# Gate and up projections of a feed-forward: 256 weight columns with weights stationary, against 512 columns token by token with a transposed product

## The chip, the cores and the metric

The kernel runs on one core of one Trainium2 chip. Its time is the device time of one execution in microseconds (us), a median over runs; the profile shows one execution. TensorE (PE) multiplies into PSUM, ScalarE (ACT) and VectorE (DVE) read PSUM and SBUF, GpSimd (POOL) works here on SBUF alone, and SyncE (SP) issues most DMAs. Each engine takes its instructions in a fixed order.

## The reference

Two layers over x of 256 tokens by 1024 features, in float32. Each layer has a feed-forward, a mixer and a second feed-forward:

```python
def swiglu(x, w_gate, w_up, w_down):
    return (jax.nn.silu(x @ w_gate) * (x @ w_up)) @ w_down

for l in range(DEPTH):                      # DEPTH = 2
    x = x + 0.5 * swiglu(rmsnorm(x, ffn1_norm[l]), ffn1_gate[l], ffn1_up[l], ffn1_down[l])
    ...                                     # h @ w_in, three token mixers, gates, w_out: x = x + merged @ w_out
    x = x + 0.5 * swiglu(rmsnorm(x, ffn2_norm[l]), ffn2_gate[l], ffn2_up[l], ffn2_down[l])
```

Gate and up are 1024 by 2816, down is 2816 by 1024. So four feed-forwards run, each with 8.65 million weights read once from HBM.

## The kernel before

**Numbers in two parts.** Each float32 operand is split into a rounded high part and a low rest. `mm3` (L105 to L108) makes one product from three matmuls: high by high, high by low, low by high. The first operand of each is stationary in the array, the second moves through it.

**Weights as units.** `units` lists all weight blocks in the order of use, 512 KB each. `load_unit` (L206) issues the DMA of one into a `raw` buffer (four of them, RB); `emit_unit` (L213) makes `wh` on ScalarE (L221) and `wl = raw - wh` on VectorE (L228; in other parts of the program GpSimd takes a share at L225 or L230). Five buffers hold `wh` and five `wl` (WB_); the last four units of a feed-forward have their own four, `xh` and `xl`. `unit()` asks for four units ahead.

**The feed-forward** (`ffn`, L332) goes in steps of 256 of the 2816 columns, eleven steps, `NB`. Step 0 has tokens stationary (`tok_mm`), and its product is transposed on TensorE (L361). Every later step calls `chan_mm` (L303) for gate and for up: the weights are stationary, 128 columns at a time, and all 256 tokens move, so the result has columns on the partitions. A unit is used by 24 matmuls in a row and then free. ScalarE takes silu out of PSUM (L367), VectorE multiplies by up (L369), ScalarE and GpSimd split the product into `ah` (L370) and `al` (L371). The down product (`rows_mm`, L315) of step j - 2 follows, 512 columns at a time, into four PSUM accumulators `pt` and `sc`. The PSUM tag `mm` has two buffers, `p2` and `y` one each.

**What sets the order.** The program is written in one order, and a list scheduler with a cost model of its own places instructions on each engine by priority; weight splits have a raised one. During the first feed-forward of a layer `side(j)` emits pieces of the setup of the S5 mixer (`setup_s5_layer`, L509): VectorE products at L568 to L592, GpSimd products at L584 and L586, some transposes and DMAs.

## Time and profile before

| | |
|---|---|
| median of 3 runs | 1356.99 us (1355.2 to 1362.29) |
| the profiled execution | 1357.2 us, of it the span from first to last instruction 1355.4 us |
| granted TensorE clock | 0.996 of full speed over the span |
| busy: PE, PE weight loads | 1331.6 us, 1256.8 us |
| busy: DVE, ACT, POOL | 826.8, 699.8, 465.3 us |
| HBM | 244.92 MB read, 194 GB/s over the span |

Busy time of PE counts each matmul from start to a modelled end, and matmuls overlap in the array, so a matmul shown with 0.28 us may be followed by the next 0.12 us later. What one matmul costs in a dense stream is the distance from its start to the start of the next. In a row for a window stand its length, then the busy time and count of PE, weight loads, DVE, ACT and POOL, then the granted clock, the busy share of the DMA engines and GB/s.

### The profile page before, as it was taken

Reading aid. Unit: us, or ns where it says so; the run is one execution under the profiler, and the core shown is the slowest. Engines: PE = TensorE matmul, PEld = TensorE weight load, DVE = VectorE, ACT = ScalarE, POOL = GpSimd, SP = SyncE. Lnnn points to the kernel's source line nnn. Section 1 sums busy time; section 2 is a strip of 40 time slices with the busy share of each in tenths; the row PEclk is TensorE's granted clock in tenths of the full one; section 3 lists DMA queues with packets and bytes.
Section 4 is the critical chain, followed back from the end, with each engine's and each line's share of the span. In section 5 each row is a group of like instructions: output and inputs, shape, how many; then the busy total and the mean of one; then the engine's idle time right before and its main releaser. Section 6 shows DMA issues by size and latency. Waiting matters only on the chain.

```text
span 1355.4 us, 25390 instructions
## 1 busy us (share of the span) xinstructions
PE 1331.6 (98%) x10120; PEld 1256.8 (93%) x10120; DVE 826.8 (61%) x1172; ACT 699.8 (52%) x1020; POOL 465.3 (34%) x333
## 2 busy tenths in 40 slices
PE   8999999999999999999999999999999999999998
PEld 7999988999999989999999999889999999899997
DVE  5696755996433665444675586569864337544443
ACT  5444445677644544444544444457766355544442
POOL 1442565454246531111122247254532555111110
PEclk9999999999999999999999999999999999999999
DMA  8866688666657556666756677766766576466662
GB/s 249 224 188 214 223 267 235 198 184 191 184 134 226 172 171 204 186 187 187 236 154 203 202 231 240 243 201 176 194 193 178 157 221 194 155 188 186 186 187 94
DMA packets 246326, 265.68 MB, mean 196 GB/s; under 512 B 51136, under 2 KB 224192, under 8 KB 246208
## 3 DMA queue, kind: packets, MB, share of 16 engines
q1 hardware_dynamic: 244400, 260.40, 64.7%
q10 hardware_dynamic: 1808, 3.67, 0.8%
q8 instruction: 79, 1.29, 0.4%
q14 instruction: 39, 0.32, 0.1%
HBM read 244.92 MB, written 18.58 MB: 194 GB/s over the span
## 4 chain that ended last, share of the span: by engine, by line
PE 76%; DVE 9%; DMA 7%; POOL 3%; ACT 2%; issue 2%; SPq 0%; ACTq 0%; DVEq 0%; POOLq 0%
PE mm L108 17%; PE mm L106 17%; PE mm L107 17%; PE pt L108 3%; PE pt L107 3%; PE pt L106 3%; DVE wl L228 3%; PE sc L108 3%; PE sc L107 3%; PE sc L106 3%; DMA raw<-in_w_in_dram 2%; DMA raw<-in_ffn_down_dram 1%; DMA raw<-in_ffn_gate_dram 1%; DMA raw<-in_ffn_up_dram 1%; PE pt L820 1%
## 5 line engine op out<-in xcount | busy, mean ns | idle before, releaser
L228 DVE TENSOR_TENSOR wl<-raw,wh 128x1024 fp32r<-128x1024 f32 (+3 forms) x376 | 443.5, 1186 | 340.8 <-ACT wh L221 327.2
L221 ACT ACTIVATE wh<-raw 128x1024 fp32r<-128x1024 f32 (+2 forms) x396 | 414.2, 1048 | 453.8 <-PE mm L107 240.8
L108 PE MATMUL mm<-hTh,wl 128*128 128x256 f32 x1728 | 490.7, 284 | 0.0
L107 PE MATMUL mm<-hTl,wh 128*128 128x256 f32 x1728 | 490.7, 284 | 0.0
L106 PE MATMUL mm<-hTh,wh 128*128 128x256 f32 x1728 | 489.0, 283 | 0.0
L106 PEld LDWEIGHTS mm<-hTh,wh 128*128 128x128 f32 x1728 | 326.5, 189 | 2.2
L108 PEld LDWEIGHTS mm<-hTh,wl 128*128 128x128 f32 x1728 | 325.9, 189 | 0.6 <-issue 0.3
L107 PEld LDWEIGHTS mm<-hTl,wh 128*128 128x128 f32 x1728 | 325.2, 188 | 1.3 <-issue 0.3
L371 POOL TENSOR_TENSOR al<-aa,ah 128x512 fp32r<-128x512 f32 x40 | 71.3, 1781 | 456.8 <-ACT ah L370 456.8
L230 POOL TENSOR_TENSOR wl<-raw,wh 128x384 fp32r<-128x384 f32 (+2 forms) x108 | 144.9, 1347 | 174.7 <-ACT wh L221 142.3
L106 PE MATMUL mm<-wh,hTh 128*128 128x256 f32 (+1 forms) x496 | 142.9, 290 | 0.0
L107 PE MATMUL mm<-wl,hTh 128*128 128x256 f32 (+1 forms) x496 | 141.8, 288 | 0.0
L108 PE MATMUL mm<-wh,hTl 128*128 128x256 f32 (+1 forms) x496 | 140.6, 288 | 0.0
L107 PEld LDWEIGHTS mm<-wl,hTh 128*128 128x128 f32 x496 | 94.1, 190 | 1.2 <-issue 0.3
L106 PEld LDWEIGHTS mm<-wh,hTh 128*128 128x128 f32 x496 | 94.0, 190 | 1.1 <-issue 0.3
L108 PEld LDWEIGHTS mm<-wh,hTl 128*128 128x128 f32 x496 | 93.1, 189 | 1.0 <-issue 0.3
L225 POOL TENSOR_TENSOR wl<-raw,wh 128x512 fp32r<-128x512 f32 x40 | 56.5, 1434 | 53.7 <-ACT wh L221 48.4
L107 PE MATMUL pt<-wl,ah 128*128 128x512 f32 x144 | 56.4, 392 | 0.0
L108 PE MATMUL pt<-wh,al 128*128 128x512 f32 x144 | 56.4, 391 | 0.0
L108 PE MATMUL sc<-wh,al 128*128 128x512 f32 x144 | 56.3, 391 | 0.0
L106 PE MATMUL pt<-wh,ah 128*128 128x512 f32 x144 | 56.2, 390 | 0.0
L107 PE MATMUL sc<-wl,ah 128*128 128x512 f32 x144 | 56.1, 390 | 0.0
(311 smaller groups left out, 2074.7 us busy)
## 6 DMA issues: line engine op xcount, KB each, us to landing
raw<-in_w_in_dram SPq DMA_DIRECT2D x100, 512.0 KB, 4.3
raw<-in_ffn_gate_dram SPq DMA_DIRECT2D x88, 512.0 KB, 4.4
raw<-in_ffn_up_dram SPq DMA_DIRECT2D x88, 512.0 KB, 4.7
raw<-in_ffn_down_dram SPq DMA_DIRECT2D x88, 512.0 KB, 4.3
raw<-in_w_out_dram SPq DMA_DIRECT2D x16, 512.0 KB, 4.2
Gd<-xh SPq DMA_DIRECT2D x8, 512.0 KB
Ad<-xl SPq DMA_DIRECT2D x8, 512.0 KB, 5.6
x<-Ad SPq DMA_DIRECT2D x8, 512.0 KB, 5.3
```

The lines of the kernel that those rows point to most:

```text
L106: PE.matmul(o, lh, rh, start=start, stop=False)
L107: PE.matmul(o, lh, rl, start=False, stop=False)
L108: PE.matmul(o, ll, rh, start=False, stop=stop)
L221: A.activation(hv, r, AF.Copy)
L225: G.tensor_tensor(lv[:, :, cs], r[:, :, cs], hv[:, :, cs].bitcast(F32), op=ALU.subtract)
L228: V.tensor_tensor(lv[:, :, :c], r[:, :, :c], hv[:, :, :c].bitcast(F32), op=ALU.subtract)
L230: G.tensor_tensor(lv[:, :, c:], r[:, :, c:], hv[:, :, c:].bitcast(F32), op=ALU.subtract)
L371: G.tensor_tensor(al, a, ah.bitcast(F32), op=ALU.subtract)
L820: PE.transpose(pt[:, i * P:(i + 1) * P], s[:, (b0 + i) * P:(b0 + i + 1) * P], ident)
```

## The change

Step 0 of a feed-forward stays, but its transposed product is split per token block through two PSUM tiles `p2` in place of one `y`. The other 2560 columns go in five blocks of 512 (`NJ`). A unit of gate or up is now 256 rows of 512 columns (it was 512 rows of 256 columns, the same 512 KB). `wide_tok` takes four units at once: for each block of 128 tokens, tokens are stationary and 512 weight columns move, 24 matmuls into one `mm` tile. Silu and product have the same shapes as before. The product now has tokens on the partitions, so `turned` transposes it on TensorE, four 128x128 pieces for a token block, into `p2`; ScalarE makes `ah` out of PSUM and VectorE `al`, which GpSimd made before. Down of block j - 1 follows with the four units of its rows, first token block 0, then token block 1. `side` is called eleven times, where it was twelve.

```diff
+    def wide_block(w, c0):
+        for k in range(0, KD, 2):
+            units.append(kview(w, c0, 512)[:, k:k + 2, :])
...
+    def wide_tok(h):
+        us = [unit() for _ in range(4)]
+        for t in range(2):
+            tk = slice(t * P, (t + 1) * P)
+            pq = ps("mm")
+            for kk in range(KD):
+                wh, wl = us[kk // 2]
+                mm3(pq, h[0][:, kk, tk], h[1][:, kk, tk], wh[:, kk % 2, :], wl[:, kk % 2, :], kk == 0, kk == KD - 1)
+            yield pq
...
-                else:
-                    pg = chan_mm(h)
-                    A.activation(s, pg, AF.Silu)
-                    pu = chan_mm(h)
-                    V.tensor_tensor(a, pu, s, op=ALU.mult)
-                    A.activation(ah, a, AF.Copy)
-                    G.tensor_tensor(al, a, ah.bitcast(F32), op=ALU.subtract)
...
-            if 1 < j < NB:
-                us = [unit(), unit()]
-                for t in range(2):
-                    down(j - 2, t, us)
-            side(j)
...
+        def turned(j, a, t, n, tag):
+            pt = ps(tag)
+            for c in range(n):
+                PE.transpose(pt[:, c * P:(c + 1) * P], a[:, c * P:(c + 1) * P], ident)
+            p3 = pt[:, :n * P].rearrange("p (c t) -> p c t", c=n)
+            ah, al = (b[:, :, t * P:(t + 1) * P] for b in at[j])
+            A.activation(ah, p3, AF.Copy)
+            V.tensor_tensor(al, p3, ah.bitcast(F32), op=ALU.subtract)
...
+        for j in range(1, NJ + 1):
+            at[j] = tb([P, 4, SEQ], F32R, "ah", 2), tb([P, 4, SEQ], F32R, "al", 2)
+            ss, aa = [], []
+            for pq in wide_tok(h):
+                ss.append(tb([P, 512], F32, "silu", 2))
+                A.activation(ss[-1], pq, AF.Silu)
+            side(2 * j - 1)
+            for t, pq in enumerate(wide_tok(h)):
+                aa.append(tb([P, 512], F32, "aa", 2))
+                V.tensor_tensor(aa[t], pq, ss[t], op=ALU.mult)
+            turned(j, aa[0], 0, 4, "p2")
+            us = [unit() for _ in range(2 if j == 1 else 4)]
+            down(j - 1, us, 0)
+            turned(j, aa[1], 1, 4, "p2")
+            down(j - 1, us, 1)
+            side(2 * j)
```

The order of instructions is the scheduler's, so it is shown at three places, with the tile numbers in the names. The first is TensorE in the second feed-forward of layer 0, at the end of an up product (`mm_`) and the start of down (`pt_`, `sc_`). Before:

```order
L106 MATMUL mm_1052_6437<-hTh_958_5851,wh_1047_6378 128x256
L107 MATMUL mm_1052_6437<-hTl_959_5852,wh_1047_6378 128x256
L108 MATMUL mm_1052_6437<-hTh_958_5851,wl_1048_6379 128x256
L106 MATMUL pt_997_6073<-wh_1050_6408,ah_999_6075 128x512
L107 MATMUL pt_997_6073<-wl_1051_6409,ah_999_6075 128x512
L108 MATMUL pt_997_6073<-wh_1050_6408,al_1000_6076 128x512
L106 MATMUL sc_996_6072<-wh_1050_6408,ah_999_6075 128x512
```

With the change, at the end of the second token block of up:

```order
L106 MATMUL mm_1075_5980<-wh_1062_5931,hTh_959_5414 128x512
L107 MATMUL mm_1075_5980<-wl_1063_5932,hTh_959_5414 128x512
L108 MATMUL mm_1075_5980<-wh_1062_5931,hTl_960_5415 128x512
L362 MATMUL p2_1077_6007<-ident_4_67,aa_1074_5978 128x128 x4
L107 MATMUL pt_999_5639<-wl_1066_5938,ah_1001_5641 128x512
L108 MATMUL pt_999_5639<-wh_1065_5937,al_1002_5642 128x512
L107 MATMUL sc_998_5638<-wl_1066_5938,ah_1001_5641 128x512
L108 MATMUL sc_998_5638<-wh_1065_5937,al_1002_5642 128x512
L106 MATMUL pt_999_5639<-wh_1068_5943,ah_1001_5641 128x512
L106 MATMUL sc_998_5638<-wh_1068_5943,ah_1001_5641 128x512
```

The matmuls have 512 columns where they had 256, the weights have become the moving operand, and four transposes (L362) of the first token block's product stand ahead of down.

The second place is TensorE a little later, from the end of down (before) or the first unit of the next gate product (with the change). Before, one unit follows another:

```order
L106 MATMUL sc_996_6072<-wh_1054_6440,ah_999_6075 128x512
L107 MATMUL sc_996_6072<-wl_1055_6441,ah_999_6075 128x512
L108 MATMUL sc_996_6072<-wh_1054_6440,al_1000_6076 128x512
L106 MATMUL mm_1069_6541<-hTh_958_5851,wh_1057_6470 128x256
L107 MATMUL mm_1069_6541<-hTl_959_5852,wh_1057_6470 128x256
L108 MATMUL mm_1069_6541<-hTh_958_5851,wl_1058_6471 128x256
```

With the change, wh_1082 is the first unit and wh_1085 the second; mm_1105 is token block 0 and mm_1107 token block 1:

```order
L108 MATMUL mm_1105_6119<-wh_1082_6022,hTl_960_5415 128x512
L106 MATMUL mm_1105_6119<-wh_1085_6028,hTh_959_5414 128x512
L106 MATMUL mm_1107_6146<-wh_1082_6022,hTh_959_5414 128x512
L107 MATMUL mm_1107_6146<-wl_1083_6023,hTh_959_5414 128x512
L108 MATMUL mm_1107_6146<-wh_1082_6022,hTl_960_5415 128x512
```

Token block 1 now begins on the first unit when token block 0 has used only the high part of the second, and token block 0 goes on behind it.

The third place is VectorE in the first feed-forward of layer 0, among the S5 products. Before (L568 to L570 and L590 are S5 products, L369 is the product with up):

```order
L228 TENSOR_TENSOR wl_174_926<-raw_158_849,wh_173_925 128x1024
L569 TENSOR_TENSOR s5Q_191_1084<-xh_192_1085,xl_193_1086 128x64x4
L570 TENSOR_TENSOR s5Q_191_1084<-xh_192_1085,xl_193_1086 128x64x4
L228 TENSOR_TENSOR wl_177_956<-raw_161_882,wh_176_955 128x1024
L228 TENSOR_TENSOR wl_181_988<-raw_164_888,wh_180_987 128x1024
L228 TENSOR_TENSOR wl_184_1018<-raw_172_923,wh_183_1017 128x1024
L228 TENSOR_TENSOR wl_187_1051<-raw_175_953,wh_186_1050 128x1024
L369 TENSOR_TENSOR aa_170_921<-mm_178_984,silu_169_920 128x512
L228 TENSOR_TENSOR wl_190_1057<-raw_179_985,wh_189_1056 128x1024
L228 TENSOR_TENSOR wl_203_1122<-raw_182_1015,wh_202_1121 128x1024
L228 TENSOR_TENSOR wl_206_1152<-raw_185_1048,wh_205_1151 128x1024
L590 TENSOR_TENSOR xh_222_1285<-s5C0_139_734,s5Q_191_1084 128x1024
```

With the change the lines are 20 higher for the same S5 products (L588 to L590, L610), L235 is the weight split and L392 the product with up:

```order
L235 TENSOR_TENSOR wl_154_684<-raw_116_530,wh_153_683 128x1024
L588 TENSOR_TENSOR xh_193_912<-s5Q_192_911,lam_6_74 128x512
L588 TENSOR_TENSOR xl_194_913<-s5Q_192_911,lam_6_74 128x512
L235 TENSOR_TENSOR wl_157_690<-raw_146_669,wh_156_689 128x1024
L235 TENSOR_TENSOR wl_164_750<-raw_149_675,wh_163_749 128x1024
L589 TENSOR_TENSOR s5Q_192_911<-xh_193_912,xl_194_913 128x64x4
L590 TENSOR_TENSOR s5Q_192_911<-xh_193_912,xl_194_913 128x64x4
L235 TENSOR_TENSOR wl_167_756<-raw_152_681,wh_166_755 128x1024
L610 TENSOR_TENSOR xh_217_1026<-s5C0_140_649,s5Q_192_911 128x1024
L610 TENSOR_TENSOR xh_256_1239<-s5C0_140_649,s5Q_192_911 128x1024
L235 TENSOR_TENSOR wl_170_762<-raw_155_687,wh_169_761 128x1024
L392 TENSOR_TENSOR aa_175_796<-mm_174_771,silu_159_718 128x512
```

Ahead of the product with up stand six S5 rows and five splits here, where two S5 rows and five splits stood before; two of the six are the long L610.

## Rows read from the trace of the kernel before

**Rows 1.** The page, part 1: busy us, share of span and count by engine:
```profile
PE 1331.6 (98%) x10120; PEld 1256.8 (93%) x10120; DVE 826.8 (61%) x1172; ACT 699.8 (52%) x1020; POOL 465.3 (34%) x333
```

**Rows 2.** The page, part 4: the chain that ended last, by engine:
```profile
PE 76%; DVE 9%; DMA 7%; POOL 3%; ACT 2%; issue 2%; SPq 0%; ACTq 0%; DVEq 0%; POOLq 0%
```

**Rows 3.** A window of 17 us in the second feed-forward, layer 0 (us; then engines):
```profile
538.00:555.00 17.00, 17.00 (x122) 16.02 (x121) 8.04 (x8) 7.37 (x9) 1.81 (x1) 1.00 0.64 186
```

**Rows 4.** Timeline of TensorE there, one step: start us, us, instruction:
```profile
537.43 0.28 PE L106 MATMUL mm<-hTh,wh 128*128 128x256 f32 x1
...
548.95 0.39 PE L106 MATMUL pt<-wh,ah 128*128 128x512 f32 x1
...
554.43 0.28 PE L106 MATMUL mm<-hTh,wh 128*128 128x256 f32 x1
```

**Rows 5.** Timeline of TensorE, 24 down matmuls of a first feed-forward, first and next:
```profile
138.97 0.39 PE L106 MATMUL pt<-wh,ah 128*128 128x512 f32 x1
...
144.41 0.28 PE L106 MATMUL mm<-hTh,wh 128*128 128x256 f32 x1
```

**Rows 6.** Timeline of TensorE, 452-column matmuls of the mixer, first and last of 14:
```profile
222.79 0.37 PE L106 MATMUL y<-wh,hTh 128*128 128x452 f32 x1
...
225.47 0.36 PE L107 MATMUL y<-wl,hTh 128*128 128x452 f32 x1
```

**Rows 7.** Timeline of TensorE, eight transposes of a norm and what follows:
```profile
219.83 0.60 PE L278 MATMUL y<-ident,xn 128*128 128x128 f32 x4
220.27 0.60 PE L278 MATMUL p<-ident,xn 128*128 128x128 f32 x4
220.62 0.45 PE L106 MATMUL mm<-wh,hTh 128*128 128x452 f32 x1
220.91 0.37 PE L107 MATMUL mm<-wl,hTh 128*128 128x452 f32 x1
```

**Rows 8.** Timeline of TensorE, a pause in the first feed-forward:
```profile
42.87 0.28 PE L108 MATMUL mm<-hTh,wl 128*128 128x256 f32 x1
44.99 0.34 PE L438 MATMUL y<-ident,sp_raw 64*128 64x64 f32 x2 [1.84 <-DVE smT L406]
```

**Rows 9.** Waits of TensorE and of its weight loads (total us, times, longest):
```profile
PE pt L106 <- ACT ah L370: 0.5, 2, 0.3
PEld pt L108 <- POOL al L371: 1.1, 2, 0.5
```

**Rows 10.** The page, part 5: weight split (L228, L221) and product split (L371):
```profile
L228 DVE TENSOR_TENSOR wl<-raw,wh 128x1024 fp32r<-128x1024 f32 (+3 forms) x376 | 443.5, 1186 | 340.8 <-ACT wh L221 327.2
L221 ACT ACTIVATE wh<-raw 128x1024 fp32r<-128x1024 f32 (+2 forms) x396 | 414.2, 1048 | 453.8 <-PE mm L107 240.8
...
L371 POOL TENSOR_TENSOR al<-aa,ah 128x512 fp32r<-128x512 f32 x40 | 71.3, 1781 | 456.8 <-ACT ah L370 456.8
```

**Rows 11.** The tile ah: its low part split out of PSUM, ns min/median/max:
```profile
L364 DVE TENSOR_TENSOR al<-y,ah x4: 675/679/681, 33.6 to 1181.5; 128x512 fp32r<-128x512 f32 x4
```

**Rows 12.** Timeline of GpSimd and VectorE around 79 and 700 us:
```profile
79.19 2.07 POOL L584 TENSOR_TENSOR xh<-s5b,s5Q 128x1024 f32<-128x1024 f32 x1 [4.03 <-DVE s5Q L569]
...
79.36 10.37 DVE L228 TENSOR_TENSOR wl<-raw,wh 128x1024 fp32r<-128x1024 f32 x4
...
699.62 5.25 DVE L228 TENSOR_TENSOR wl<-raw,wh 128x1024 fp32r<-128x1024 f32 x2
```

**Rows 13.** Groups by shape: VectorE's 128x1024 forms (count, busy us, mean ns):
```profile
L228 DVE TENSOR_TENSOR wl<-raw,wh 128x1024 fp32r<-128x1024 f32 x262 | 340.6, 1307 | 260.8 <-ACT wh L221 253.9 <-PE mm L108 4.3
...
L590 DVE TENSOR_TENSOR xl<-s5C,s5Q 128x1024 f32<-128x1024 f32 x8 | 22.9, 2866 | 0.2 <-ACT s5C L576 0.2
```

**Rows 14.** Waits of ScalarE and of SyncE's queue:
```profile
ACT wh L221 <- PE mm L107: 240.8, 154, 3.0
SPq L210 <- DVE wl L228: 663.9, 309, 16.7
```

**Rows 15.** The page, part 6: weight loads, KB each, us to landing:
```profile
raw<-in_ffn_gate_dram SPq DMA_DIRECT2D x88, 512.0 KB, 4.4
```

More of the change, by code (lines that the diff above doesn't have):

```diff
@@ L35 @@
 DFF = 2816
-NB = DFF // 256
+NJ = (DFF - 256) // 512
 W = 256
@@ L134, in ffn_stream @@
         g, u, d = I[f"ffn{f}_gate"][l], I[f"ffn{f}_up"][l], I[f"ffn{f}_down"][l]
-        for j in range(NB + 1):
-            if j < NB:
-                deep_block(g, 256 * j)
-                deep_block(u, 256 * j)
-            if 1 < j < NB:
-                row_block(d, 256 * (j - 2))
-            if j == NB:
-                row_block(d, 256 * (NB - 2), True)
-                row_block(d, 256 * (NB - 1), True)
+        deep_block(g, 0)
+        deep_block(u, 0)
+        for j in range(NJ):
+            wide_block(g, 256 + 512 * j)
+            wide_block(u, 256 + 512 * j)
+            if j == 0:
+                row_block(d, 0)
+            else:
+                for i in range(2):
+                    row_block(d, 512 * j - 256 + 256 * i)
+        for i in range(2):
+            row_block(d, 512 * NJ - 256 + 256 * i, True)
     def mix_stream(l):
@@ L332, in ffn, with down @@
     def ffn(h, done, side):
[L333 removed]
         at = {}
[L336 to L339 removed]
+        def down(j, us, t, hfs=(0, 1)):
+            for kk, (wh, wl) in enumerate(us):
+                st, sp = (j == 0 and kk == 0), False
                 rows_mm(acc, at[j][0][:, kk, :], at[j][1][:, kk, :], t, wh, wl, st, sp, hfs)
[L342 to L378 removed]
@@ L379, in ffn @@
-        u9, u10 = [unit(), unit()], [unit(), unit()]
+        def turned(j, a, t, n, tag):
[6 more added lines that the diff above has]
+            V.tensor_tensor(al, p3, ah.bitcast(F32), op=ALU.subtract)
+        at[0] = tb([P, 2, SEQ], F32R, "ah0"), tb([P, 2, SEQ], F32R, "al0")
@@ new lines, in ffn @@
+        us = [unit() for _ in range(4)]
+        pgu = [ps("mm") for _ in range(2)]
+        for t in range(2):
+            tok_mm(h, [t], us[:2], 256, pgu[0])
+            tok_mm(h, [t], us[2:], 256, pgu[1], None if t else h[2])
+        s, a = (tb([P, 2, SEQ], F32, n, 2) for n in ("silu", "aa"))
+        with tc.high_priority():
+            for t in range(2):
+                A.activation(s[:, t], pgu[0][:, t * 256:(t + 1) * 256], AF.Silu)
+                V.tensor_tensor(a[:, t], pgu[1][:, t * 256:(t + 1) * 256], s[:, t], op=ALU.mult)
+            for t in range(2):
+                turned(0, a[:, t], t, 2, "p2")
@@ new lines, in ffn @@
+        side(0)
+        acc = acc4()
+        for j in range(1, NJ + 1):
[14 more added lines that the diff above has]
+            side(2 * j)
@@ L380, in ffn @@
+        us = [unit() for _ in range(4)]
         tr = None
@@ L382, in ffn @@
             for hf in range(2):
-                down(NB - 2, t, u9, (hf,))
-                with behind(tr if hf else None):
-                    down(NB - 1, t, u10, (hf,))
+                for kk, (wh, wl) in enumerate(us):
+                    with behind(tr if hf and kk > 1 else None):
+                        rows_mm(acc, at[NJ][0][:, kk, :], at[NJ][1][:, kk, :], t, wh, wl, False, kk == 3, (hf,))
                 tr = update(acc, t, hf, done) or tr
```

31 lines of the change are left out of this document (removed).

## The prediction, made before the changed kernel was run

> **What bounds the kernel now.** The page's first part comes first: TensorE is busy 98% of the span, VectorE and ScalarE far less [rows 1]. The chain that ended last says the same: 76% of it is TensorE's own work, 7% DMA [rows 2]. Busy time of matmuls overlaps, though, so the next view is the windows. In the second feed-forward of layer 0 one step of 256 columns takes 17.0 us, with TensorE busy for all of it at a granted clock of 1.00 (2.4 GHz), VectorE for 8.0 us, ScalarE for 7.4 and the DMA engines 0.63 [rows 3]. The timeline of that step, read by starts, shows what the time is made of: 96 gate and up matmuls of 256 columns from 537.43 to 548.95, 0.1200 us each, and 24 down matmuls of 512 columns from there to 554.43, 0.2283 us each [rows 4]. Nothing stands between them. A feed-forward is a stream of matmuls, and its time is their number by their spacing. Weights are no limit there: ScalarE waited 240.8 us for TensorE to free a weight buffer [rows 14], so units are ready early.
>
> **Fewer, longer matmuls.** Ten steps in four feed-forwards, 96 matmuls each, are 3840 matmuls of 256 columns: 460.8 us. The change does the same products in 1920 matmuls of 512 columns. At the spacing of the down product they take 1920 x 0.2283 = 438.4 us, a gain of 22.4 us. Twice 0.1200 less 0.2283 is 0.012 us, the fixed part of one matmul that each pair saves. The trace has no gate product in the new form, tokens stationary and 512 weight columns moving. The nearest in size is the down product. The nearest in form is the mixer's projection with tokens stationary and 452 columns moving: 13 distances from 222.79 to 225.47 are 0.206 us each [rows 6], by its columns 0.2335 for 512. Then the new matmuls take 448.3 us and the gain is 12.5. I take the down product, since it has the very width, and keep 12.5 as the poor end. The good end is 0.2267: 24 down matmuls of a first feed-forward, from 138.97 to 144.41 [rows 5], which gives 25.5.
>
> **Added transposes.** Five blocks by eight 128x128 transposes in four feed-forwards are 160 (step 0 had its four already). Eight transposes of a norm start at 219.83, the matmul of 452 columns behind them at 220.62, and its successor at 220.91 [rows 7]. From 219.83 to 220.91 is 1.08 us, less 0.206 for the one matmul leaves 0.874, or 0.109 each. So a transpose costs nearly what a matmul of twice its columns costs, and 160 cost 17.5 us, all on TensorE. Matmuls and transposes together gain 4.9 us.
>
> The Trainium skill (TensorE: Matmul & The Clock Gate, section Back-to-back issue gap) gives the warm spacing as N / 2.4 GHz plus 2.5 ns: 55.8, 109.2 and 215.8 ns for 128, 256 and 512 columns. By that, halving the matmuls saves 1920 x 2.5 ns = 4.8 us, the transposes cost 8.9 us, and the two lose 4.1 us together. The trace has 109, 120 and 228 ns, so the rows decide.
>
> **Waits that go.** TensorE paused from 42.87 to 44.99 for small transposes of the S5 parameters, 2.0 us beyond one matmul [rows 8]. With the change these stand behind the whole first gate product, so that pause should vanish. At the ends of the first feed-forwards the last down product waited for the two splits, 0.5 us on ScalarE's and 1.1 us on GpSimd's [rows 9]. GpSimd's took 1.78 us [rows 10], VectorE's out of PSUM takes 0.68 [rows 11], and 24 matmuls of the other token block now stand ahead of its use. Together up to 3.6 us; some may return elsewhere, so I take 3, with bounds 0 and 3.6.
>
> **Work that is moved and hidden.** Forty low-part splits go from GpSimd to VectorE: 40 x 0.68 = 27 us more for VectorE. In the quiet feed-forwards it is half idle [rows 3], so this costs nothing there. The tile `p2` is single: the second four transposes wait until ScalarE and VectorE have read the first, some 1.3 us by the splits' durations, and 33 down matmuls (7.5 us) stand between. If that cover went, TensorE itself would stand, for 1.3 us forty times. Silu and product keep shapes and numbers. The weight loads stay 66 units per feed-forward on SyncE's queue, in rows of 2 KB. `side` still gives the S5 setup its nine pieces in layer 0.
>
> **Waits that are added.** Four units are now read twice, once per token block, so none is free before the second pass. Only the fifth buffer can be filled ahead. In the second pass a unit is free after each 6 x 0.2283 = 1.37 us. Its successor needs ScalarE's 1.05 and VectorE's 1.31 us [rows 10, 13], so it is ready 3.7 us into the pass at the earliest and wanted 6.8 us into it: 3.1 us of slack. Before, the four units ahead were used at 2.88 us each (24 x 0.1200), over 8 us of slack. In the two second feed-forwards nothing disturbs VectorE, and 3.1 us is enough. In the first ones S5 work does. Beside GpSimd's 128x1024 products, four weight splits took 10.37 us in layer 0 and two took 5.25 in layer 1 [rows 12]: 5.1 and 2.6 us over the usual. An S5 product of VectorE takes 2.87 us [rows 13], and in the third order shown two of them stand in a row between two splits. At that place TensorE should lose 2 us for the slow splits and 2.6 for the pair (5.7 less 3.1), and all matmuls behind wait with it. In layer 1 the excess of 2.6 is within the slack. I take 5 us in all. The low end is 0, if the S5 work falls where units are ready. The high end is 2 us at each of the eight quarters of S5 setup, 16 us.
>
> **Sum.** -22.4 + 17.5 - 3 + 5 = -2.9 us. The profiled execution took 1357.2 us, 1355.4 of them in the span, so 1354.3; it lies 0.2 us above the median of the runs shown, and I forecast 1354 us. Its own range is 1349 to 1361. About 0.5%, 6.8 us, is what a measurement of this kernel can tell from no change: faster is below 1350.2, slower above 1363.8.
>
> **Rivals.** *A, the S5 work costs nothing.* Without the 5 us and at the good spacing: -25.5 + 17.5 - 3.6 = -11.6, 1345.6 us. For it: in the trace the same slow splits never stopped TensorE, and a list scheduler can put S5 work where units are not yet due. Against: they had over 8 us of slack there.
>
> *B, each hand-over of four units waits.* Slower than before, if loads set the pace. SyncE's queue waits for VectorE's split to free a `raw` buffer, 663.9 us in all [rows 14], so a load starts only when a split ends, and four now end in a burst. A buffer goes round in load, 1.05 and 1.31 us, and four buffers must go round once per 24 + 24 matmuls, 10.9 us. So loads may take 8.5 us before TensorE stands. Against it: they land in 4.4 us [rows 15], and even at the mean 186 GB/s of the window [rows 3], 2.8 us a unit, the fourth load of a burst, issued 4.1 us after the first, lands in 7.1. From 8.5 us on it decides. With loads of 9 us it costs 0.5 us at each of some 60 hand-overs: 1357.2 - 4.9 - 3 + 30 = 1379 us.
>
> *C, the new form spaces like the 452-column product.* -12.5 + 17.5 - 3 + 5 = +7.0, 1364 us. For it: the same form, on the same engine. Against: the down product, at the full width, keeps 0.228 in every feed-forward. (The skill's spacing rule, named above, points the same way.)
>
> **How the numbers follow.** Forecast 0.55, A 0.25, B 0.12, C 0.08. Faster by over 0.5%: A and a little of the forecast's low end, 0.30. Slower: B and most of C, 0.19, and the forecast's high end adds 0.01: 0.20. Within 0.5%: 0.50. The range takes in A's time and C's, and on the high side stops within B: 1345 to 1369 us.
>
> **What would show it.** Starts of gate matmuls 0.227 to 0.230 us apart, and transposes 0.109, confirm the first two terms; 0.233 is C. A block of 512 columns in the second feed-forward should take 2 x 48 x 0.2283 + 0.87 + 48 x 0.2283 = 33.7 us where two steps took 34.0. New pauses of TensorE should lie between 60 and 105 us, with VectorE's split as the releaser; none at all is A. Pauses at each hand-over in the second feed-forwards, released by a split that waited for a DMA, are B, and the forecast is wrong. It is also wrong if the mixer, which the change does not touch, moves by more than 2 us because the scheduler orders it anew.

## The result and the profile after

The changed kernel takes 1370.09 us (median of 4 runs, 1367.86 to 1371.23), the kernel before in the same session 1358.17 (1355.2 to 1362.29): a ratio of 1.0095, interval 1.0072 to 1.0118. It is about 1% slower. The forecast was 1354 us and its range ended at 1369. The profiled execution spans 1368.3 us at a mean granted clock of 0.991 (before 1355.4 and 0.996), so 12.9 us are to be explained.

The page of the changed kernel, busy time and chain by engine, answers [rows 1, 2]:

```profile
PE 1341.6 (98%) x8360; PEld 1176.2 (86%) x8360; DVE 849.4 (62%) x1216; ACT 700.5 (51%) x1024; POOL 406.5 (30%) x293
...
PE 81%; DVE 9%; DMA 4%; ACT 2%; issue 2%; POOL 2%; SPq 0%; POOLq 0%; DVEq 0%; ACTq 0%
```

TensorE has 1760 instructions fewer (1920 matmuls fewer, 160 transposes more) and is as busy as ever. To see where the time went, the span is cut at the first transpose of each norm. Worked out from the traces, in us:

| | FFN 1, layer 0 | mixer | FFN 2 | FFN 1, layer 1 | mixer | FFN 2 |
|---|---|---|---|---|---|---|
| before | 205.25 | 281.13 | 188.99 | 197.63 | 280.58 | 194.24 |
| changed | 208.52 | 280.09 | 190.33 | 205.50 | 280.79 | 195.57 |

The mixers moved by -1.0 and +0.2. Every feed-forward became longer: the second ones, where nothing disturbs VectorE, by 1.3 each, the first ones by 3.3 and 7.9. These are stages of one profiled execution each. The second feed-forwards repeat within 0.7 us where nothing in them is changed (189.00 and 194.49 in e14 below, which has them as before; 190.95 and 195.62 in e6, which has them as changed). For the whole, the time of one kernel moves with the granted clock: the kernel before, run 29 times in one session, took 1353.02 us at 0.997 and 1362.45 at 0.988.

**The undisturbed loss.** The timeline of TensorE in the second feed-forward of layer 1, the counterpart of [rows 4]: the first and the 49th gate matmul of a block, and the first of the next block.

```profile
1250.96 0.40 PE L106 MATMUL mm<-wh,hTh 128*128 128x512 f32 x1
...
1262.11 0.40 PE L106 MATMUL mm<-wh,hTh 128*128 128x512 f32 x1
...
1285.16 0.40 PE L106 MATMUL mm<-wh,hTh 128*128 128x512 f32 x1
```

11.15 us for 48 steps are 0.2323 each, where I had taken the 0.2283 of the down product. A block takes 34.20 us; I had said 33.7, against 34.0 for the two steps it replaces. Five blocks make 1.0 of the 1.3 us. No wait stands in between.

**The largest new wait.** It lies in the first feed-forward of layer 1. The timeline of ScalarE and VectorE, then that of TensorE (in brackets the idle time before an instruction and its releaser), then windows with the busy time of PE, PEld, DVE, ACT and POOL, the granted clock and the DMA's share:

```profile
706.27 0.38 ACT L365 ACTIVATE ah<-p 128x256 fp32r<-128x256 f32 x1 [0.93 <-PE p L362]
703.07 5.24 DVE L235 TENSOR_TENSOR wl<-raw,wh 128x1024 fp32r<-128x1024 f32 x2
708.23 2.04 DVE L591 TENSOR_TENSOR s5D<-s5D,cm 128x128 f32<-128x128 f32 x1
710.20 6.32 DVE L610 TENSOR_TENSOR xh<-s5C,s5Q 128x1024 f32<-128x1024 f32 x2
716.45 0.41 DVE L366 TENSOR_TENSOR al<-p,ah 128x256 fp32r<-128x256 f32 x1
```

```profile
705.86 0.38 PE L362 MATMUL p<-ident,aa 128*128 128x128 f32 x2
...
712.85 0.49 PE L595 MATMUL y<-ident,s5c 128*128 128x128 f32 x3
716.91 0.44 PE L362 MATMUL p<-ident,aa 128*128 128x128 f32 x2 [3.57 <-DVE al L366]
```

```profile
713.00:717.00 4.00, 0.43 (x5) 0.20 (x3) 4.00 (x4) 1.54 (x2) 3.92 (x2) 1.00 0.00 0
...
718.00:721.50 3.50, 3.50 (x9) 2.33 (x8) 3.50 (x3) 0.35 (x1) 0.75 (x1) 0.53 0.18 32
```

The second pair of transposes of step 0 waits for the single tile `p2`, which the views call `p`. That tile is free when the 0.41 us split at 716.45 has read it. ScalarE's copy of the tile had ended at 706.65; the split then stood 9.8 us in VectorE's queue, behind two weight splits of 2.6 us each, beside which GpSimd ran, and three S5 products. TensorE had 29 gate matmuls and three S5 transposes to do meanwhile, 705.99 to 713.34, and stood still for the rest. After the pause the clock is granted at about half (0.53; 1.2 GHz is one half) for 3.5 us, with 9 matmuls in a window in which the next one has 16.

**Other waits of TensorE** (in total us, times, longest), to hold against [rows 9]:

```profile
PE p L362 <- DVE al L366: 3.6, 1, 3.6
...
PE sc L106 <- DVE x L342: 2.9, 3, 2.1
...
PE mm L107 <- DVE wl L235: 1.2, 1, 1.2
```

The pause for `smT` [rows 8] is gone, as forecast. Three of these waits, in the timeline of TensorE: for a weight split in the first feed-forward of layer 0, at the end of the same one for the update of x, and at the norm behind the first feed-forward of layer 1.

```profile
144.70 0.50 PE L107 MATMUL mm<-wl,hTh 128*128 128x512 f32 x1 [1.23 <-DVE wl L235]
213.37 0.50 PE L106 MATMUL sc<-xh,ah 128*128 128x512 f32 x1 [2.12 <-DVE x L342]
891.96 0.66 PE L285 MATMUL y<-ident,xn 128*128 128x128 f32 x4 [0.93 <-DVE xn L281]
```

The end of the first feed-forward of layer 0 now waits for the update of x, where before it waited for the splits.

### The profile page after: what moved, and what is told of

Read it like the earlier page. It is cut to its first block, busy times and chain, and to the rows that moved or that the text cites. A ratio compares the mean times of both kernels' runs of the same rounds, so it can differ in the third digit from the quotient of the medians.

```text
span 1368.3 us, 21779 instructions
## 1 busy us (share of the span) xinstructions
PE 1341.6 (98%) x8360; PEld 1176.2 (86%) x8360; DVE 849.4 (62%) x1216; ACT 700.5 (51%) x1024; POOL 406.5 (30%) x293
## 4 chain that ended last, share of the span: by engine, by line
PE 81%; DVE 9%; DMA 4%; ACT 2%; issue 2%; POOL 2%; SPq 0%; POOLq 0%; DVEq 0%; ACTq 0%
PE mm L106 18%; PE mm L108 18%; PE mm L107 18%; DVE wl L235 3%; PE pt L107 3%; PE pt L108 3%; PE pt L106 3%; PE sc L108 3%; PE sc L106 3%; PE sc L107 3%; PE p L362 1%; PE pt L840 1%; PE y L966 1%; PE y L964 1%; DMA raw<-in_ffn_gate_dram 1%
## 5 line engine op out<-in xcount | busy, mean ns | idle before, releaser
L235 DVE TENSOR_TENSOR wl<-raw,wh 128x1024 fp32r<-128x1024 f32 (+3 forms) x376 | 459.8, 1232 | 292.8 <-ACT wh L228 285.6
L228 ACT ACTIVATE wh<-raw 128x1024 fp32r<-128x1024 f32 (+2 forms) x396 | 412.8, 1048 | 389.7 <-PE mm L108 185.7
L106 PE MATMUL mm<-wh,hTh 128*128 128x512 f32 (+1 forms) x1136 | 396.8, 353 | 0.2 <-ACT hTh L289 0.2
L107 PE MATMUL mm<-wl,hTh 128*128 128x512 f32 (+2 forms) x1136 | 395.3, 351 | 1.6 <-DVE wl L235 1.2
L108 PE MATMUL mm<-wh,hTl 128*128 128x512 f32 (+1 forms) x1136 | 394.6, 350 | 0.0
L107 PEld LDWEIGHTS mm<-wl,hTh 128*128 128x128 f32 x1136 | 216.5, 191 | 30.9 <-DVE wl L235 2.3
L108 PE MATMUL mm<-hTh,wl 128*128 128x256 f32 x448 | 126.7, 283 | 0.0
L107 PE MATMUL mm<-hTl,wh 128*128 128x256 f32 x448 | 126.6, 283 | 0.0
L106 PE MATMUL mm<-hTh,wh 128*128 128x256 f32 x448 | 126.4, 282 | 0.0
L107 PEld LDWEIGHTS mm<-hTl,wh 128*128 128x128 f32 x448 | 84.3, 188 | 0.3 <-issue 0.3
L108 PEld LDWEIGHTS mm<-hTh,wl 128*128 128x128 f32 x448 | 84.3, 188 | 0.3 <-issue 0.3
L106 PEld LDWEIGHTS mm<-hTh,wh 128*128 128x128 f32 x448 | 84.4, 188 | 0.0
L392 DVE TENSOR_TENSOR aa<-mm,silu 128x512 f32<-128x512 f32 x40 | 27.4, 686 | 48.4 <-PE mm L108 48.4
```

Source lines behind the costliest of these rows:

```text
L106: PE.matmul(o, lh, rh, start=start, stop=False)
L107: PE.matmul(o, lh, rl, start=False, stop=False)
L108: PE.matmul(o, ll, rh, start=False, stop=stop)
L228: A.activation(hv, r, AF.Copy)
L235: V.tensor_tensor(lv[:, :, :c], r[:, :, :c], hv[:, :, :c].bitcast(F32), op=ALU.subtract)
L392: V.tensor_tensor(aa[t], pq, ss[t], op=ALU.mult)
```

## The experiments

Every ratio is to the kernel before, run on the same chip in the same session.

**e1, streams of TensorE alone.** Is the 0.232 made by 24 matmuls in a row into one PSUM bank?

```diff
+ for j, (k, i) in enumerate(every):      # L111: one bank for 24
+     PE.matmul(o[r % 2], *terms(k)[i], start=j == 0, stop=j == 23)
...                                       # L116, L121, L127: bank changed every 3, 1, 6
+ for j in range(24):                     # L130: one bank, operands fixed
+     PE.matmul(o[2 + r % 2], *terms(0)[0], start=j == 0, stop=j == 23)
```

> The kernel holds nothing but ten streams of TensorE work on operands that lie in SBUF, each on its own line, with no other engine and no DMA at work beside them; it leaves out everything else that the two kernels compute. In the changed kernel the gate and up matmuls start 0.232 us apart and the down matmuls of the same 512 columns 0.227. Theory, the bank: a gate or up pass puts 24 matmuls in a row into one bank of PSUM, the down product three. Then the stream of 24 in a row and the one with a single stationary and a single moving operand, both in one bank, are spaced 0.232 us, the streams that change the bank after three (also with fixed operands) and after every one 0.227, after six between them; 452 columns in one bank 0.206; 256 columns with weights stationary 0.120 in one bank and a few ns less where the bank changes. Rival one, the neighbours: the gate passes lose 5 ns to reads and writes of other engines, and here all streams of 512 columns show 0.227. Rival two, the operands: fixed operands give 0.227, changing ones 0.232, whatever the bank. Transposes 0.109 in all of them.

Grouped by line: durations, and the first and last start in us.

```profile
L116 PE MATMUL b<-wh,hl x48: 389/389/389, 60.5 to 92.5; 128*128 128x512 f32 x48
...
L130 PE MATMUL b<-wh,hh x144: 389/389/389, 153.5 to 185.9; 128*128 128x512 f32 x144
```

The one-bank stream takes 32.4 us for 143 steps, 0.2266; the one that changes the bank every three, 32.0 for 141, 0.2270. Median distances of all streams of 512 columns were 226 or 227 ns, of 452 columns 0.2065 and of 256 columns 0.120. The bank has no part in it, and 452 columns cost 0.2065 with nothing beside them.

**e2, no transposes.**

```diff
-            pt = ps(tag)
-            for c in range(n):
+            pt = ps(tag) if j == 0 else a
+            for c in range(n if j == 0 else 0):
                 PE.transpose(pt[:, c * P:(c + 1) * P], a[:, c * P:(c + 1) * P], ident)
```

> The changed kernel without the 160 transposes of blocks 1 to 5: the two parts of the product are split straight from its tile in SBUF, untransposed, so what the down product reads is in another layout; step 0 keeps its four transposes and its wait in layer 1. Theory: a transpose takes 0.109 us of TensorE and nothing else hangs on them, so the time falls by 160 x 0.109 = 17.5 us, to 1352 or 1353 us. Rival: the passage through the single tile p2 makes waits that the sum did not have (the splits read PSUM, the down product waits for them), and the time falls by 20 us or more. Other rival: what is left of the loss is on other engines and the time falls by less than 14.

1363.33 us, ratio 1.0052 (1.0032 to 1.0072): only some 6 us less, the last case of the expectation. By stage (us, order of the table): 207.89, 281.09, 186.55, 205.94, 280.78, 190.71. Against the changed kernel the second feed-forwards are 3.8 and 4.9 us shorter, 8.6 for 80 transposes: 0.108 each, as priced. The first ones are 0.6 shorter and 0.4 longer: with 4.4 us less to do, TensorE only waited more.

```profile
PE sc L106 <- DVE x L342: 7.2, 4, 3.3
...
PE pt L107 <- DVE wl L235: 4.3, 4, 1.7
PE p L362 <- DVE al L366: 3.6, 1, 3.6
```

So in the first feed-forwards TensorE is no longer what sets the end; VectorE is.

**e3, step 0 through one tile.**

```diff
-            for t in range(2):
-                turned(0, a[:, t], t, 2, "p2")
+            pt = ps("y")                      # four transposes of both tokens, then
+            A.activation(at[0][0], p3, AF.Copy)
+            V.tensor_tensor(at[0][1], p3, at[0][0].bitcast(F32), op=ALU.subtract)
```

> The changed kernel with step 0 put through one PSUM tile with four transposes, one copy and one low-part split for both tokens, as the kernel before does it; blocks 1 to 5 stay. Theory: in layer 1 TensorE stands 3.6 us because the second pair of transposes of step 0 waits for the tile p2, whose split is queued on VectorE behind two weight splits slowed by GpSimd's products and two products of the S5 setup; the granted clock then falls to one half for 3.4 us, which costs another 1.4. With one tile nothing is behind that split but the first down product, 24 us later: the time falls by 4 to 5.5 us, and there is no stretch at half clock near 718 us. Rival: the wait comes back at the next matmul that needs a weight split queued on VectorE behind the same S5 products; then the time falls by less than 2 us.

1373.85 us, ratio 1.0122 (1.0095 to 1.0148): no gain. In layer 1 the theory held: the first feed-forward took 201.86 us, 3.6 less, with no pause at the tile and no half clock. In layer 0 it took 213.07, 4.5 more. The order of VectorE had shifted, and weight splits came late behind S5 products, three times between 81 and 89 us (of all 4.0 us):

```profile
PE pt L107 <- DVE wl L235: 4.0, 3, 1.5
```

The rival was right about the kind of wait: in layer 1 it came back small, 0.3 and 1.4 us at 722 and 726 us, and large in layer 0, where the expectation had not looked for it.

**e4, unit by unit.**

```diff
-            for kk in range(KD):
-                wh, wl = us[kk // 2]
+        for i in range(4):
+            wh, wl = unit()
+            for t in range(2):                # both token blocks, then the next unit
+                for k in range(2):
```

> The changed kernel with gate and up read unit by unit: both token blocks use a unit before the next one comes, in two PSUM banks, six matmuls in each by turns; so a unit is free after 12 matmuls instead of after the second pass, and the bank changes every six matmuls instead of every 24. Step 0 is as in the changed kernel. Theory, the bank: the spacing falls from 0.232 towards 0.228, at 5 ns less for one matmul in six some 1 to 2 ns, 2 to 4 us in all over 1920. Theory, the supply: the pauses of TensorE behind slow weight splits in the first feed-forwards (1.2 us at 143 us) go. Together 1364 to 1368 us. Rival: neither matters, the spacing stays at 0.232, and the time at 1370.

1381.34 us, ratio 1.0182 (1.0158 to 1.0205). No expectation had this time. The spacing stayed at 0.232, as the rival had it. A unit free earlier did not help: the first feed-forwards took 215.53 and 211.41 us, with a pause of 3.2 us in layer 0 and the old one of 3.6 in layer 1, each with a stretch at half clock behind it. The pause of 3.6 us is no longer than in the changed kernel, so it does not explain the 5.9 us more in layer 1. There TensorE goes over from gate matmuls to small S5 matmuls 18 times, in the changed kernel 3 times; what that costs was not separated.

```profile
PE p L363 <- DVE al L367: 3.6, 1, 3.6
...
PE p L107 <- DVE wl L235: 3.2, 1, 3.2
```

**e5, the splits alone, in the kernel before.**

```diff
-                    G.tensor_tensor(al, a, ah.bitcast(F32), op=ALU.subtract)
+                    V.tensor_tensor(al, a, ah.bitcast(F32), op=ALU.subtract)
```

> The kernel before with one part of the change alone: the low-part split of the product (40 of them) stands on VectorE instead of GpSimd; layout, weight units and matmuls are those of before. Theory, supply: what the change loses in the first feed-forwards is lost because VectorE has no time left there while the S5 setup runs and because a unit that is read twice leaves 3 us of slack instead of 8; with the slack of before, 0.7 us more on VectorE per step moves nothing: the same time within 0.3%, 1354 to 1359 us, and no pause of TensorE between 60 and 105 us or 700 and 750 us. Rival, the splits alone: VectorE's 27 us more are enough to fill it, and this kernel shows pauses of TensorE of 1 us and more behind weight splits in these stretches and is 3 to 8 us slower than before.

1358.51 us, ratio 1.0009 (0.9995 to 1.0024): the same. One pause came, 1.8 us in layer 1, for the product `aa` and not for a weight split. By stage the profiled execution is less even: the first feed-forwards took 207.48 and 200.28 us, 2.2 and 2.7 more than before, and the mixers 279.50 and 276.06, 1.6 and 4.5 less. In the first feed-forwards stretches at half clock (46 and 719 us) are part of it; why the mixers are shorter stays open. The 27 us more on VectorE do not make the whole slower by themselves; that they cost the first feed-forwards nothing is not shown.

**e6, no large S5 products.**

```diff
-            for i, o in enumerate((f4, m4)):
-                G.tensor_tensor(o, b[i]..., Qt[:, i, 1, gs]..., op=ALU.mult)
-            G.tensor_tensor(F, F, m1, op=ALU.add)
...
+            G.memset(F, 0.5)
+            V.memset(H, 0.5)
```

> The changed kernel with the S5 setup's large products left out: the three 128x1024 operations of GpSimd and the three of VectorE in each of four quarters are one fill each, so the numbers that the S5 part later reads are not its own; everything else stands. Theory, supply: the second feed-forwards, which have no such work, lost 1.3 us each to the change, the first ones 3.3 and 7.9; without the products the first ones lose 1.3 us each too, all pauses behind weight splits and the one of 3.6 us behind the tile p2 go, and with them the half clock at 718 us: some 8 us less than the changed kernel, 1361 to 1363 us. Rival, the form itself: what the first feed-forwards lose hangs on their other work (the transposes and small matmuls of the setup, which stay), and the time falls by less than 3 us.

1364.7 us, ratio 1.0054 (1.0036 to 1.0073): 0.0041 less than the changed kernel, 5.6 us. The first feed-forwards took 206.54 and 201.04 us; TensorE waited neither for the tile `p2` nor for a VectorE split of weights there, and behind the start of the program (before 17 us) no matmul of them ran at half clock. That these products make the waits is shown; it is less than the 8 us expected, and 1.3 and 3.4 us stayed. The run takes out GpSimd's products and VectorE's together, so how much each of them does (the slowed splits, or the full queue) is not separated.

**e7, the places of the operands.** Streams alone again, at the addresses of the changed kernel.

```diff
+ HH, HL, WH, WL, AH, AL = 47552, 55744, 64064, 84544, 117312, 125504
+ gate(0, HH, HL, WH, WL)       # L125: gate form, its own places
+ down(0, AH, AL, WH, WL)       # L128: down form, its own places
+ gate(0, AH, AL, WH, WL)       # L131;  down(0, HH, HL, WH, WL)  # L134
+ ...                           # L137 all + 64, L140 stationary + 64, L143 moving + 64,
+                               # L146 all + 4096, L149 stationary - 16384
```

> Again streams of TensorE work alone, 96 matmuls of 512 columns each, now with operands at the very places in SBUF that the changed kernel gives them: gate form and down form at their own places; the gate form with the stationary operand where the down product has it, and the reverse; the gate form with everything, with the stationary operand alone and with the moving operand alone 64 bytes further on; with everything 4096 bytes further on; and with the stationary operand 16384 bytes nearer. It leaves out all the rest. The first streams kernel had 0.2267 us for every stream of 512 columns, so the 0.232 of the gate passes is not the bank. Theory, the places: the gate form at its own places shows 0.232, the down form 0.227, and the reversed places reverse it; one of the shifts brings the gate form to 0.227. Rival, the company: all nine streams show 0.227, and the 0.232 comes with what else runs in the kernel or with the program around the matmuls.

The timeline of TensorE; a stream's length is the next one's start less its own, over 96:

```profile
58.68 21.93 PE L128 MATMUL b<-big 128*128 128x512 f32 x96
80.44 21.93 PE L131 MATMUL b<-big 128*128 128x512 f32 x96
102.21 22.48 PE L134 MATMUL b<-big 128*128 128x512 f32 x96
124.52 22.46 PE L137 MATMUL b<-big 128*128 128x512 f32 x96
146.82 22.14 PE L140 MATMUL b<-big 128*128 128x512 f32 x96
168.80 22.56 PE L143 MATMUL b<-big 128*128 128x512 f32 x96
191.20 22.47 PE L146 MATMUL b<-big 128*128 128x512 f32 x96
213.51 22.47 PE L149 MATMUL b<-big 128*128 128x512 f32 x96
```

The form does not matter, the place does: with the stationary operand where the down product has it, the two forms take 21.76 and 21.77 us, 0.2267 a step (L128, L131); where the gate product has it, 22.31 us, 0.2324 (L134, and the median of L125 is 0.232). Moving all by 64 or 4096 bytes changes nothing; moving the stationary one alone by 64 gives 0.2290, the moving one alone 0.2333. So it is the distance between the two. In the changed kernel `hTh` lies 16512 bytes ahead of the first `wh`, 128 more than 16384.

**e8, a gap of 384 bytes** makes that distance 16896, a multiple of 512. Apart from one fill the order on every engine is the same.

```diff
+        if not gap:
+            gap.append(sb([P, 96], F32, "gap"))
+            G.memset(gap[0], 0.0)
```

> The changed kernel with one tile of 384 bytes per partition, filled once, between the normed activations and the weight tiles. Every instruction stands in the same order; only the weights lie 384 bytes further from the activations, 16896 bytes instead of 16512, so that the distance is a multiple of 512. Theory, the places: the streams kernel had 0.2267 us for a gate matmul whose stationary and moving operands lie a multiple of 512 bytes apart and 0.232 for those of the changed kernel, so 1920 matmuls gain 5.5 ns each, 10.6 us, and the time falls to 1359 or 1360 us; the second feed-forwards, where TensorE sets the pace, gain 2.6 us each, and the first ones gain less where VectorE sets it, so 1364 us at the worst. Rival: with DMA and three other engines at work the 0.232 has other causes too, and the time falls by less than 3 us.

1366.55 us, ratio 1.0053 (1.0034 to 1.0073): 0.0042 or 5.7 us less. Fifty steps of the gate product in the second feed-forward of layer 1:

```profile
1216.37 0.39 PE L108 MATMUL mm<-wh,hTl 128*128 128x512 f32 x1
...
1227.71 0.39 PE L106 MATMUL pt<-wh,ah 128*128 128x512 f32 x1
```

11.34 us, 0.2268 each. The second feed-forwards took 187.56 and 192.81 us, 2.8 less each, as expected, and 1.4 less than before the change. The first ones took 207.48 and 204.58, only 1 us less each. In layer 0 the first 48 matmuls took 0.8 us more than in the changed kernel; in layer 1 the pause at the tile stayed (3.8 us), and the stretch at half clock behind it lasted 6 us where it had been 3.5.

**e9, the same gap in the kernel before.** The edit is that of e8.

> The kernel before with the same tile of 384 bytes in the same place and every instruction in the same order. Theory, the places: its feed-forward products move the activations 256 columns at a time at 0.120 us, which the first streams kernel also had with the operands a multiple of 512 bytes apart, so the feed-forwards stay; only the mixer's projections with tokens stationary can gain. The same time as before within 0.3%. Rival: the 256-column products are spaced by places too, and the time falls by 4 us or more.

1360.02 us, ratio 1.0021 (1.0003 to 1.0038): no gain; the feed-forwards with 256 columns have nothing to win. Its second feed-forwards took 0.2 us more each, the first one of layer 0 3.0 more. Half of that 3.0 is the clock: the order of instructions is that of before, and so is the pause of 1.8 us for `smT` [rows 8], but here a stretch at half clock follows it. Windows behind the pause, in the kernel before and in e9:

```profile
45.00:48.50 3.50, 3.50 (x29) 3.43 (x30) 2.21 (x3) 1.03 (x2) 0.99 (x1) 1.00 1.06 233
...
46.00:49.50 3.50, 3.50 (x19) 3.43 (x18) 2.23 (x5) 1.50 (x3) 0.75 (x1) 0.53 0.87 210
```

A further 0.5 us was lost in the first 48 matmuls. So a stage of one execution can be 1.5 us longer with nothing changed in the program. Why the median of ten runs came out a little higher stays open.

**e10, gap and one tile in layer 1.** The edits of e8, and of e3 where `l == 1`.

> The changed kernel with the tile of 384 bytes and, in the first feed-forward of layer 1 alone, step 0 put through one PSUM tile for both tokens. In layer 1 that edit shortened the first feed-forward by 3.6 us, in layer 0 it lengthened it by 4.5. Theory: the two edits add, and the time is 4 us below the kernel with the gap alone, 1355 to 1356 us, level with the kernel before (1357). Rival, supply: with the faster gate matmuls TensorE meets the weight splits queued on VectorE earlier, the pause comes back there, and the time is within 1.5 us of the kernel with the gap alone.

1363.11 us, ratio 1.0025 (1.0004 to 1.0046): 3.8 us less than e8 by the ratios, but the intervals overlap, so that the whole is faster than e8 is not shown. The first feed-forward of layer 1 took 202.06 us, 2.5 less than in e8. The pause of 3.8 us at the tile and the half clock behind it are gone, and TensorE waits more for weight splits (1.7 us in e8):

```profile
PE mm L107 <- DVE wl L235: 3.7, 4, 1.4
```

Both theories have a share. This is the lowest median of the complete change, and it isn't below that of the kernel before.

**e11, ten distances.**

```diff
+ for dlt in (0, 32, 64, 96, 128, 192, 256, 320, 384, 448):
+     gate(0, WH - 16384 + dlt, WH - 8192 + dlt, WH, WL)    # L136 to L163
+ chan(...); narrow(...)                                    # 256 columns, L166 to L175
```

> TensorE alone again: 96 gate matmuls of 512 columns for each of ten distances between the stationary and the moving operand in SBUF, 16384 bytes less 0, 32, 64, 96, 128, 192, 256, 320, 384 and 448; then 256 columns with the weights stationary and with the tokens stationary, at a multiple of 512 bytes and at the changed kernel's distance. It leaves out all the rest. Theory, the places: 0.2267 at a distance of 0, and from the second streams kernel 0.2289 at 64 bytes short of it, 0.2324 at 128 and 0.2333 at 192 on the other side; with the sign turned round I expect some of these shifts near 0.227 and others at 0.232 to 0.233. For 256 columns 0.120 at both distances. Rival: the distance is not what counts but the place of one operand, and then shifts of the stationary operand alone show 0.227 at all ten.

```profile
57.87 22.55 PE L139 MATMUL b<-big 128*128 128x512 f32 x96
80.26 22.56 PE L142 MATMUL b<-big 128*128 128x512 f32 x96
102.66 22.64 PE L145 MATMUL b<-big 128*128 128x512 f32 x96
125.14 22.46 PE L148 MATMUL b<-big 128*128 128x512 f32 x96
147.43 22.14 PE L151 MATMUL b<-big 128*128 128x512 f32 x96
169.41 21.92 PE L154 MATMUL b<-big 128*128 128x512 f32 x96
191.17 22.56 PE L157 MATMUL b<-big 128*128 128x512 f32 x96
213.56 22.47 PE L160 MATMUL b<-big 128*128 128x512 f32 x96
235.88 22.14 PE L163 MATMUL b<-big 128*128 128x512 f32 x96
257.86 23.18 PE L166 MATMUL b<-big 128*128 128x256 f32 x192
280.87 22.95 PE L169 MATMUL b<-big 128*128 128x256 f32 x192
303.66 11.67 PE L172 MATMUL b<-big 128*128 128x256 f32 x96
```

Read as in e7, the spacing is 0.2332, 0.2333, 0.2342, 0.2322 and 0.2290 us at shifts of 32, 64, 96, 128 and 192 bytes, 0.2267 at 256, and then the same again: 0.2332, 0.2325, 0.2290 at 320, 384 and 448. It repeats every 256 bytes. For 256 columns with the weights stationary it was 0.1198 at a multiple of 512 (L166) and 0.1187 at the changed kernel's distance (L169).

**e12, the new form in the second feed-forwards alone,** with the gap: the first ones are those of the kernel before.

```diff
-            ffn(h[0], nt, step(gs, l))
+            ffn_narrow(h[0], nt, step(gs, l))     # the function before; its units as well
```

> The first feed-forward of each layer as in the kernel before, the second one as in the changed kernel, and the tile of 384 bytes between activations and weights; nothing is left out. Theory: with the gap the second feed-forwards of the changed kernel took 187.6 and 192.8 us where the kernel before took 189.0 and 194.2, and everything else is that of before, so the time is 2.8 us below before, 1354 to 1355 us at before's 1357.5. Rival: the gains of the form are lost again beside it (the mixers and first feed-forwards drift by as much), and the time is within 1 us of before or above it.

1358.34 us (5 rounds), ratio 1.0009 (0.9994 to 1.0024): no difference from before. The second feed-forwards took 188.44 and 192.82 us, 0.6 and 1.4 less than before; the first one of layer 1 took 200.07, 2.4 more, with a wait that before did not have:

```profile
PE pt L107 <- ACT ah L464: 2.1, 1, 2.1
```

The rival was right. A gain of 2 us is smaller than what moves when the scheduler lays the program out anew.

**e13 and e14, without the S5 products: the changed kernel with the gap, and the kernel before.** The edits are those of e6 and e8.

> The changed kernel with both edits: the tile of 384 bytes, and the large products of the S5 setup replaced by fills, so that the numbers of the S5 part are not its own. Theory: the two add. Against the changed kernel the gap gives 5.5 us where VectorE holds the first feed-forwards back and up to 10.6 where it does not, and the missing products 5.6, so the ratio to before falls from 1.0095 to between 0.998 and 1.001, 1354 to 1359 us. Rival: TensorE, now faster, meets other waits in the first feed-forwards and the time stays above 1361.

> The kernel before without the large products of the S5 setup, replaced by fills as in the changed kernel, so that the numbers of the S5 part are not its own. Theory: with more than 8 us of slack nothing in its feed-forwards waits for these products, so its time moves by less than 2 us, 1355 to 1358. Rival: they cost it as much as the changed kernel, and it falls by 4 to 6 us, to 1352.

e13: 1356.96 us, ratio 0.9998 (0.9982 to 1.0015). e14: 1357.47 us, ratio 0.9998 (0.9982 to 1.0014). Both theories held. The kernel before loses nothing to these products; the changed one loses 0.0055 to them with the gap (e8 against e13). With both causes taken away, the whole 0.0095 is gone, but the whole gains nothing either.

## Why the prediction was wrong

**The spacing of the new matmuls: wrong, 7.6 us.** I put 1920 at 0.2283, the down product's, "since it has the very width". They take 0.2323: 446.0 us instead of 438.4, a gain of 14.8 instead of 22.4. The rows I used were right for the down product; what sets 0.2267 or 0.2324 is the distance between stationary and moving operand in SBUF (e7, e11), and the down product's `ah` happened to lie well, `hTh` 128 bytes off. Rival C had the number (0.2335) for another reason: the 452 columns take 0.2065 alone (e1), and that the form makes it is refuted by e7. C's price came true without C's cause, and I had given it 0.08. With the gap the second feed-forwards gain 1.4 us each (e8), near the 1.2 that the first two terms give for one feed-forward (4.9 over four; 2.0 with the 0.2268 of e8).

**The transposes: right.** 160 x 0.109; e2 measured 0.108.

**The added waits: the size about right, by luck; the place and the price wrong.** I took 5 us, between 0 and 16; the S5 products cost the changed kernel 5.6 us (e6), 7.5 with the gap (e8, e13). But I looked for them in layer 0 between 60 and 105 us and called layer 1 "within the slack"; there was no pause there in layer 0, and 7.9 us went in layer 1. The step that failed is the one on the single tile `p2`: "some 1.3 us by the splits' durations, and 33 down matmuls (7.5 us) stand between". A cover stood between in step 0 of layer 1 too, 29 gate matmuls and three transposes, 7.3 us in all. What was wrong is the 1.3 us: the split needs 0.41, but it waited 9.8 us for its turn in VectorE's queue, and TensorE stood for 3.6. In the second feed-forwards the same split waited 1.0 us at most. The half clock behind the pause adds to the price: seven steps between matmuls took 3.25 us where 0.232 each makes 1.6.

**Splits to VectorE cost nothing: right for the whole time of the kernel before (e5).** In the changed kernel they share a queue that, beside the S5 products, is full: between 70 and 80 us VectorE, the third of the busy times in this window, is busy for 10.0 of 10 us.

```profile
70.00:80.00 10.00, 10.00 (x45) 8.13 (x44) 10.00 (x11) 4.28 (x5) 8.21 (x2) 1.00 0.76 239
```

**Waits that go: half right.** The 2.0 us for `smT` went. The end of the first feed-forward of layer 0 gave nothing back: a wait of 2.1 us for the update of x stands there instead. Without S5 products and with the gap, the first feed-forwards took 205.52 and 198.24 us (e13) against 205.25 and 197.63 before and 203.93 and 197.42 in the kernel before without these products (e14), where the form should have gained 1.2 each and these waits 3 in all.

**The mixers: right,** within 2 us.

Put together by the terms of the sum: -14.8 + 17.5 - 2.0 + 5.6 = +6.3 of the 12.9 us. The two edits of e13 account for all of it, to within its interval (about 2.3 us either way). For the two profiled executions the waits shown above close most of what is left. In layer 0 the first feed-forward lost 1.3 as the second ones, 1.2 at 144.70 and 2.1 at 213.37, 0.5 by its first 48 matmuls, and got back 2.0 for `smT`: 3.1 of 3.3. In layer 1 it lost 1.3, 3.6 at the tile, 1.6 at half clock and 0.9 at 891.96: 7.4 of 7.9. These waits are not independent; where one is removed another comes (e2, e3, e10).

Rival A fell, with 13 us lost. Rival B, a hand-over that waits each time, did too: in the second feed-forwards no wait stands within a block.

## What to carry to other kernels

A spacing read from one matmul holds for another of the same shape only if their operands lie alike in SBUF: look up the addresses, and if matmuls of 512 float32 columns have an activation tile and weight tiles that are not a multiple of 256 bytes apart, try a pad (with 256 columns it won nothing, e9). Where a step is "covered" by other work, set the cover against the time until the step gets its turn in its engine's queue, and not against its own duration alone, and do so at each of its occurrences. And remove work from the engine you take for the bound in one stage: if the time stays, as in e2, the bound is another.

## What the runs showed of the hardware

- Matmuls of 512 float32 columns with a new stationary operand each start 0.2267 us apart when stationary and moving operand lie a multiple of 256 bytes apart, and up to 0.2342 at other distances (e11); the bank, the order and fixed operands make no difference (e1). With 256 columns the effect has the other sign and 1.1 ns (0.1198 and 0.1187).
- The bf16 matmuls of 512 columns with fixed operands in e1 and e7 started 0.216 us apart (median of the starts in the traces). The Trainium skill (TensorE: Matmul & The Clock Gate, section Back-to-back issue gap) states N / 2.4 GHz plus 2.5 ns, 215.8 ns, as the gap of an isolated matmul: the traces agree for these, and the float32 matmuls here take 11 to 18 ns more.
- VectorE's weight split took 1.22 us at 700.60 in the changed kernel, where GpSimd stood still, and 2.6 each at 703.07, where it ran its products.
- A pause of 3.6 us on TensorE was followed by a stretch at the lower clock; the same pause in e2, e4 and e8 was too, and where it was gone, in e3, e6 and e10, so was the stretch at that place. Behind a pause of 1.8 us, at the same place of the same order of instructions, the granted clock was 0.53 in e9 and 1.00 in the kernel before.
